# Order edges on VectorE in a hybrid decoder trunk: receptance shifts, score masks and a block inverse

## The chip, the cores and the metric

The kernel runs on one core of a Trainium2 chip. The metric is the device time of one execution in microseconds (us). Before the change it is 1174.61 us, the median of three runs between 1174.42 and 1174.98. The engines are named here as in the profile: PE is TensorE (PEld its weight loads), DVE is VectorE, ACT is ScalarE, POOL is GpSimd, SP issues the DMAs.

## The reference

One decoder layer on 256 tokens of width 2048, in float32. The normed input is multiplied by `w_in`. A quarter of the result goes to a pooling mixer, the rest is shifted by one token and goes to an RWKV-7 mixer with 16 heads of 64, whose state is carried through the sequence:

```
z = rms_norm(x) @ w_in
pool_out = (causal window means of z_pool, minus z_pool) @ pool_w * pool_scale
r, k, v, ... = token_shift(z[rest], mu)          # z + (z_prev - z) * mu
per token and head:  sa = S a;  S = S * w + sa b^T + v k^T;  y = S r
y = group_norm(y) + sum(r * k * r_k) * v          # the bonus
x = x + concat(pool_out, y * g) @ w_out
x = x + relu(rms_norm(x) @ w_ffn_up)^2 @ w_ffn_down
x = x + sigmoid(rms_norm(x) @ w_ple_gate) * (p @ w_ple_proj);  out = rms_norm(x)
```

## The kernel before, in words

**Products.** Every weight is float32 and is split into a high half `wh` (a rounding copy on ScalarE, line 168) and a low half `wl` (the subtraction `raw - wh` on VectorE, line 169); activations are split alike. A product is then three matmuls: high by high (line 244), low activation by high weight (245), high activation by low weight (241). A panel is 128 rows by 1024 columns; `raw`, `wh` and `wl` have three buffers each, so the raw buffer of a panel is free for the third panel after it once its subtraction is done, and its `wl` buffer once its matmuls of line 241 are done. `gemm_toks` is a generator that loads and splits the panels and yields after each step of matmuls. Panels are named by product and number: `zp0_2` is the third of the eight panels of the first pool product.

**The RWKV mixer in chunks.** The recurrence over 256 tokens is done in four chunks of 64 for two groups of eight heads (`gi` 0 and 1). For each group: `rwkv_lora`, `rwkv_k` and `rwkv_r` make the decayed keys, `AR` and `BK`; `rwkv_scores` multiplies them into four groups of scores c0 to c3 (line 672), each in two PSUM banks, and multiplies these by a mask into `SC` (line 679, two instructions for a group); `inverse` inverts triangular blocks of the scores on VectorE; `rwkv_merge` makes two more block products (`gm` and `qm`, line 767) from the inverse's results; `rwkv_values` turns and centres the values (`vt`, line 790), copies them into `UV` (line 793) and makes the bonus; `rwkv_core` runs the recurrence.

**The inverse** is a generator too. It forms `AT`, then takes 31 steps of a multiplication and an addition on `X` (lines 734 and 738), then transposes blocks of `X` into `T1G` (two at line 742), copies (two at 745), transposes back into `X` (two at 749), and ScalarE copies `X` into the scores (line 753). In the first group its tiles `AT`, `X` and `tmp` use the buffers `q0`, `q1` and `q2`. `T1G` takes `q0` when `AT` is done with it, and is read by `gm` and `qm`. The two tiles of `UV` use `q0` and `q1`, so the first half of the values can be copied only when `T1G` is done with, and the second only when `X` is.

**PSUM.** Four banks of the pool "rw" serve everything of the RWKV mixer: the transposed products (`zrT` for the receptance), `vt`, the sums `bsum`, the scores, `gm`, `qm` and the recurrence. The large products have four banks of their own.

**What sets the order.** TensorE's order is that of the program as it is written, through the whole mixer part. `queue` holds the generators of the large products; `fill(us)` takes so many microseconds of their steps to lie between the steps of the RWKV mixer. The inverse of the first group is stepped beside them (`beside`, `pace`), and what is left of it is run out ahead of `rwkv_values(0, ...)`. VectorE and ScalarE are ordered by a planner when the program is built: among the instructions that its own estimate holds ready, it takes the one of highest priority, which is the earlier one in the program, unless it is raised: `high_priority(20000)` for the splits, 30000 for the copies out of PSUM such as the shifts. On the chip each engine keeps the planned order. `issue_after(ins)` puts the instructions of its block behind `ins` on the same engine; `behind` is a table of instructions that others are put behind.

**The receptance shift.** `turn` in `z_product` transposes the product into two banks and calls `shift_evac` for four column groups: ScalarE scales the bank by `1 - mu` into the tile (line 338), VectorE adds the shifted bank times `mu` (line 339).

Of the kernel before, what the change touches and what calls it, by code (L numbers as in the profile page):

```python
# [9 lines left out]
F32 = mybir.dt.float32  # L10
F32R = mybir.dt.float32r
AF = mybir.ActivationFunctionType
ALU = mybir.AluOpType
# [27 lines left out]
def trunk(  # L41
# [119 lines left out]
    def split_w(raw, name, after=None):  # L161

        wh = wp.tile([128, 1024], F32R, tag="wh", name=f"wh_{name}")
        wl = wp.tile([128, 1024], F32R, tag="wl", name=f"wl_{name}")
        with tc.high_priority(20000):
            for a in range(2):
                with tc.issue_after(after.ins) if after is not None else ExitStack():
                    nc.scalar.activation(wh[:, a * 512 : (a + 1) * 512], raw[:, a * 512 : (a + 1) * 512], AF.Copy)  # L168
            nc.vector.tensor_tensor(wl, raw, wh.bitcast(F32), op=ALU.subtract)  # L169
        return [(t_h, t_l) for t_h, t_l in zip((wh[:, 0:512], wh[:, 512:1024]), (wl[:, 0:512], wl[:, 512:1024]))]  # L170

    def split_sb(h_ap, l_ap, src_ap):
# [163 lines left out]

    def shift_evac(dst, src, mu_ap, omu_ap):
        nc.scalar.activation(dst, src, AF.Copy, scale=omu_ap)
        nc.vector.scalar_tensor_tensor(
            dst[:, 1:T], src[:, 0 : T - 1], mu_ap, dst[:, 1:T], op0=ALU.mult, op1=ALU.add  # L340
        )

# [137 lines left out]
    def z_product(i, tag, mu_name, gi, stage="a0"):  # L480

        box = []

        def consume(banks):
            if stage == "a0":
                zt = a8(0, f"{tag}{gi}s")[:, 0:1024].rearrange("p (a n) -> p a n", a=2)
            else:
                zt = rp.tile([128, 2, 512], F32, tag=stage, name=f"{tag}{gi}s")
            with tc.high_priority(30000):
                for tt in range(2):  # L490
                    nc.scalar.activation(zt[:, tt], banks[tt], AF.Copy, scale=rs1[:, tt : tt + 1])
            box.append(zt)

        def turn():
            zt = box.pop()
            dst = e4(tag)
            banks = [rw_bank(f"{tag}T{i}") for i in range(2)]
            for p in range(4):
                for tt in range(2):
                    o = p % 2 * T + tt * 128  # L500
                    nc.tensor.transpose(banks[p // 2][:, o : o + 128], zt[:, tt, p * 128 : (p + 1) * 128], ident)
            for p in range(4):
                c = PARAM_COLS[mu_name] - m0 + 4 * gi + p
                with tc.high_priority(30000):
                    shift_evac(dst[:, p, :], banks[p // 2][:, p % 2 * T : (p % 2 + 1) * T], col(mu_name, 4 * gi + p), omu[:, c : c + 1])
            return dst

        gen = queued(gemm_toks(w_in[i + gi], hT, f"{tag}{gi}", consume))

        def finished(us=1.70):  # L510
            finish(gen)
            fill(us)
            return turn()

        return finished
# [143 lines left out]
    def rwkv_scores(gi, st, cs=(0, 1, 2, 3)):  # L659

        AR, BK = st["AR"], st["BK"]
        if 0 in cs:
            st["SC"] = rp.tile([128, 2, 4, 8, 64], F32, tag="SC", bufs=2, name=f"SC{gi}")
        SC = st["SC"]
        cm = cmask.rearrange("s (k t) -> s k t", k=2)
        for c in cs:
            if c:
                fill(2.60 if gi else 4.55)
            bks = [rw_bank(f"sc{e}") for e in range(2)]
            for p in range(4):  # L670
                for e in range(2):
                    nc.tensor.matmul(
                        bks[e][:, p * 128 : (p + 1) * 128],
                        BK[e * 64 : (e + 1) * 64, p, c].rearrange("p i t -> p (i t)"),
                        AR[e * 64 : (e + 1) * 64, p, c].rearrange("p i t -> p (i t)"),
                        start=True, stop=True,
                    )
            for e in range(2):
                nc.vector.tensor_tensor(
                    SC[:, :, c].rearrange("s k (p e) t -> s k p e t", e=2)[:, :, :, e, :],  # L680
                    bks[e].rearrange("s (p k t) -> s k p t", k=2, t=64),
                    cm.unsqueeze(2).to_broadcast([128, 2, 4, 64]), op=ALU.mult,
                )

    def rwkv_sources(gi, st):

# [14 lines left out]
    def inverse(gi, st):  # L701
# [25 lines left out]
        for k in range(31):  # L727
            n, m = k // 2 + 1, 31 - k
            t_ = X.rearrange("u j t -> u (j t)")[:, 512 : 512 + n * m].rearrange("u (j t) -> u j t", t=m)
            held = {(1, 11): "state1", (1, 16): "state2"}.get((gi, k))  # L730
            while held and held not in behind:
                yield
            with tc.issue_after(behind[held].ins) if held else ExitStack():
# [4 lines left out]
            nc.vector.tensor_tensor(W[:, 0:n, k + 1 : 32], W[:, 0:n, k + 1 : 32], t_, op=ALU.add)  # L738
            yield
        T1G = rp.tile([96, 32, 32], F32, tag=tags[0], name=f"T1G{gi}")  # L740
        for i in range(2):
            nc.vector.transpose(T1G[64:96].rearrange("t u j -> t j u")[:, i::2], W[i * 64 : i * 64 + 32])
            yield
        for i in range(2):
            nc.vector.tensor_copy(tmp[0:64, i::2, :], W[i * 64 : i * 64 + 64])
            yield
        for hf in range(2):
            h = slice(hf * 16, hf * 16 + 16)
            nc.vector.transpose(X[0:64].rearrange("j u t -> j t u")[:, h], tmp[0:64].rearrange("u j t -> u t j")[:, h])
            yield  # L750
        for q in range(2):
            r = slice(q * 32, q * 32 + 32)
            nc.scalar.activation(SCu[r, :, q * 32 : q * 32 + 32], X[r], AF.Copy)
        st["T1G"] = T1G
        yield

    def rwkv_merge(gi, st):
# [22 lines left out]
        fill(4.19 if gi else 1.52)  # L780
        block_products("qm", lambda u: two(T1G[32:64, u]), lambda u: SCu[32:64, u, 32:64], SCu[0:32, :, 32:64])

    def rwkv_values(gi, st, zv):

        uvs = [rp.tile([128, 2, 8, 64], F32, tag=f"q{i}", name=f"UV{gi}_{i}") for i in range(2)]
        UV = [uvs[c // 2][:, c % 2] for c in range(4)]
        for tt in range(2):
            b = rw_bank("vt")
            for p in range(4):
                nc.tensor.matmul(b[:, p * 128 : (p + 1) * 128], zv[:, p, tt * 128 : (tt + 1) * 128], cen, start=True, stop=True)  # L790
            for i in range(2):
                with tc.high_priority(30000):
                    nc.scalar.activation(flat3(UV[2 * tt + i])[64:128], b[i * 64 : (i + 1) * 64, :], AF.Copy)
        bon = st["rk"]
        bf, vf = flat(bon), flat(zv)
        block_sum(
            st["rk"], f"rk{gi}",
            lambda hf, b: nc.vector.tensor_tensor(
                bf[:, hf * 512 : (hf + 1) * 512], b, vf[:, hf * 512 : (hf + 1) * 512], op=ALU.mult
            ),  # L800
        )
        st["UV"] = UV

    def rwkv_core(gi, st, started=None):
        AR, pc, SC, BKt, UV = st["AR"], st["pc"], st["SC"], st["BKt"], st["UV"]
# [244 lines left out]
    st1 = rwkv_lora(1)  # L1050
    rwkv_k(1, st1, z_zk1(1.33))
    rwkv_r(1, st1, z_zr1())
    run(beside.pop(0) if beside else ())
    beside.clear()
    rwkv_values(0, st0, zv0)
    make_bands()
    fill(8.39)
    rwkv_scores(1, st1)
# [18 lines left out]
    run(beside.pop(0) if beside else ())  # L1077
    beside.clear()
    rwkv_merge(1, st1)
    rwkv_values(1, st1, zv1)  # L1080


    xr = [a8(3 + tt, f"x{tt}") for tt in range(2)]
# [484 lines left out]
```

## Time and profile before

| | |
|---|---|
| median of 3 runs | 1174.61 us (1174.42 to 1174.98) |
| the profiled execution: its own time | 1175.37 us |
| the profiled execution: span of the trace | 1173.4 us, 17398 instructions |
| granted TensorE clock | 0.999 |
| HBM read | 221.19 MB, 190 GB/s over the span |

The profile is one execution. Its page gives the busy time of each engine and the chain of work that ended last. The answers of the trace used below are of two kinds. A row of waits reads: engine, what it was about to do and its line, who released it, then the total in us, how often, the longest. A row of a timeline reads: start in us from the span's start, duration, engine, line, operation, output and inputs, shapes and count; where several instructions in a row are merged, the duration runs from the first start to the last end. A bracket behind it gives the idle time of the engine ahead of it and what released it. Consecutive instructions overlap a little, so that the next one starts up to 0.1 us before the last one ends.

The stretch that the change touches lies between 155 and 190 us: the end of the first group's inverse, the second group's keys and receptance, and the second group's scores, beside the first pool product (`zp0`).

### The profile page before, as it was taken

The page shows a single profiled execution, that of the slowest core. Times are in us where ns is not written, and L with a number is a line of the kernel's source. Part 1 is how long each engine was busy: PE and PEld are TensorE (multiplying, and loading weights), DVE is VectorE, ACT ScalarE, POOL GpSimd, SP SyncE. Part 2 cuts the span into 40 slices and gives each one's busy share as a digit, 9 for nine tenths or more (in the row PEclk, how much of TensorE's full clock was granted, in tenths as well). Part 3 has the DMA queues.
Part 4 walks back from the last instruction along what each step waited for, and adds up shares of the span by engine and source line. Part 5 has one row for each costly group of instructions (what it writes and reads, how often), then busy time and mean ns, then how long its engine had stood idle before and what let it go on. Part 6 is the DMA issues. An engine that isn't in the chain of part 4 may idle for free.

```text
span 1173.4 us, 17398 instructions
## 1 busy us (share of the span) xinstructions
PE 1160.2 (99%) x6407; PEld 972.1 (83%) x6407; DVE 877.7 (75%) x1194; ACT 713.5 (61%) x1323; POOL 57.1 (5%) x133
## 2 busy tenths in 40 slices
PE   9999999999999999999999999999999999999997
PEld 8788777888888888888888888888888888888886
DVE  7686996964756666766998997676768988897543
ACT  8776849676544565555664664555556665677543
POOL 2100000000000000000110110000000110000000
PEclk9999999999999999999999999999999999999999
DMA  7454343354455555565786786555555886975511
GB/s 292 154 202 147 131 139 117 129 180 161 161 200 178 180 183 194 197 216 180 223 246 213 229 254 218 193 186 193 184 193 165 260 254 220 323 241 188 197 55 72
DMA packets 67253, 224.42 MB, mean 191 GB/s; under 512 B 7712, under 2 KB 8480, under 8 KB 66784
## 3 DMA queue, kind: packets, MB, share of 16 engines
q1 hardware_dynamic: 60240, 207.38, 51.5%
q0 software_dynamic: 6496, 15.21, 5.7%
q8 instruction: 50, 0.82, 0.3%
q10 hardware_dynamic: 432, 0.73, 0.2%
q14 instruction: 35, 0.29, 0.1%
HBM read 221.19 MB, written 2.10 MB: 190 GB/s over the span
## 4 chain that ended last, share of the span: by engine, by line
PE 96%; DVE 2%; DMA 1%; ACT 1%; issue 0%; POOL 0%; SPq 0%; DVEq 0%; POOLq 0%; ACTq 0%
PE u_w L1136 20%; PE u_w L1141 10%; PE d_b L1293 7%; PE d_b L1295 7%; PE d_b L1294 7%; PE d_w L1293 2%; PE d_w L1295 2%; PE d_w L1294 2%; PE gt_b L244 2%; PE gt_b L245 2%; PE gt_b L241 2%; PE zp_b L241 1%; PE zv_b L244 1%; PE zv_b L241 1%; PE zk_b L244 1%; PE zv_b L245 1%
## 5 line engine op out<-in xcount | busy, mean ns | idle before, releaser
L1136 PE MATMUL u_w<-h,wh_u 128*128 128x512 f32 x1024 | 321.8, 396 | 0.0
L168 ACT ACTIVATE wh_u<-raw_u 128x512 fp32r<-128x512 f32 x256 | 147.5, 624 | 162.8 <-issue 101.8
L169 DVE TENSOR_TENSOR wl_u<-raw_u,wh_u 128x1024 fp32r<-128x1024 f32 x128 | 156.7, 1224 | 104.8 <-ACT wh_u L168 103.3
L1141 PEld LDWEIGHTS u_w<-h,wl_u 128*128 128x128 f32 x1024 | 192.7, 188 | 45.1
L1141 PE MATMUL u_w<-h,wl_u 128*128 128x256 f32 x1024 | 201.2, 278 | 0.0
L1136 PEld LDWEIGHTS u_w<-h,wh_u 128*128 128x128 f32 x1024 | 156.1, 189 | 0.2
L169 DVE TENSOR_TENSOR wl_gt<-raw_gt,wh_gt 128x1024 fp32r<-128x1024 f32 x24 | 29.4, 1224 | 23.2 <-ACT wh_gt L168 23.1
L173 ACT ACTIVATE wad<-ring 128x512 fp32r<-128x512 f32 x29 | 18.2, 628 | 43.9 <-DVE ring L1344 43.9
L168 ACT ACTIVATE wh_gt<-raw_gt 128x512 fp32r<-128x512 f32 x48 | 27.9, 633 | 24.2 <-PE gt_b L245 17.0
L244 PE MATMUL gt_b<-wh_gt,h 128*128 128x512 f32 x96 | 37.4, 390 | 0.0
L245 PE MATMUL gt_b<-wh_gt,h 128*128 128x512 f32 x96 | 37.4, 390 | 0.0
L1346 DVE TENSOR_TENSOR raw_d<-raw_d,ring 128x1024 f32<-128x1024 f32 x29 | 35.5, 1223 | 0.7
L1263 POOL DMA_DIRECT2D ring<-in_w_ffn_down_dram x29 | 16.5, 568 | 362.0 <-DVE wad L174 361.3
L1264 POOL DMA_DIRECT2D ring<-in_w_ffn_down_dram x29 | 25.3, 874 | 105.5 <-DMA ring<-in_w_ffn_down_dram 105.5
L169 DVE TENSOR_TENSOR wl_o<-raw_o,wh_o 128x1024 fp32r<-128x1024 f32 x16 | 19.6, 1223 | 12.9 <-ACT wh_o L168 11.4
L168 ACT ACTIVATE wh_o<-raw_o 128x512 fp32r<-128x512 f32 x32 | 18.4, 623 | 16.3 <-issue 8.5
L168 ACT ACTIVATE wh_zp<-raw_zp 128x512 fp32r<-128x512 f32 x32 | 18.6, 623 | 15.8 <-PE zp_b L245 7.2
L169 DVE TENSOR_TENSOR wl_zk<-raw_zk,wh_zk 128x1024 fp32r<-128x1024 f32 x16 | 19.4, 1222 | 10.2 <-ACT wh_zk L168 10.2
L244 PE MATMUL zv_b<-wh_zv,hTh 128*128 128x512 f32 x64 | 26.0, 406 | 0.0
L241 PE MATMUL gt_b<-wl_gt,h 128*128 128x512 f32 x96 | 25.8, 389 | 0.0
L244 PE MATMUL zp_b<-wh_zp,hTh 128*128 128x512 f32 x64 | 25.7, 401 | 0.0
L168 ACT ACTIVATE wh_zk<-raw_zk 128x512 fp32r<-128x512 f32 x32 | 18.4, 622 | 11.9 <-DMA raw_zk<-in_w_in_dram 5.7
(927 smaller groups left out, 3014.8 us busy)
## 6 DMA issues: line engine op xcount, KB each, us to landing
raw_u<-in_w_ffn_up_dram SPq DMA_DIRECT2D x128, 512.0 KB, 4.3
raw_d<-in_w_ffn_down_dram SPq DMA_DIRECT2D x99, 512.0 KB, 4.7
ring<-in_w_ffn_down_dram POOLq DMA_DIRECT2D x58, 256.0 KB, 4.6
raw_gt<-in_w_ple_gate_dram SPq DMA_DIRECT2D x24, 512.0 KB, 4.1
raw_zk<-in_w_in_dram SPq DMA_DIRECT2D x16, 512.0 KB, 3.8
raw_zr<-in_w_in_dram SPq DMA_DIRECT2D x16, 512.0 KB, 3.2
raw_zv<-in_w_in_dram SPq DMA_DIRECT2D x16, 512.0 KB, 3.3
raw_zp<-in_w_in_dram SPq DMA_DIRECT2D x16, 512.0 KB, 3.3
```

The source lines that it names most:

```text
L168: nc.scalar.activation(wh[:, a * 512 : (a + 1) * 512], raw[:, a * 512 : (a + 1) * 512], AF.Copy)
L169: nc.vector.tensor_tensor(wl, raw, wh.bitcast(F32), op=ALU.subtract)
L241: nc.tensor.matmul(banks[tt], ah[:, ts_], halves[a][1], start=False, stop=last)
L244: nc.tensor.matmul(banks[tt], ah[:, ts_], halves[a][0], start=i + a == 0, stop=False)
L245: nc.tensor.matmul(banks[tt], al[:, ts_], halves[a][0], start=False, stop=False)
L1136: nc.tensor.matmul(bank[:, ct, :].rearrange("p (s t) -> p s t", s=2), wh[:, cs[ct]], hl, start=k == 0, stop=False, skip_group_check=True,)
L1141: nc.tensor.matmul(bank[:, ct, 0:T], wl[:, cs[ct]], hl[:, 0, :], start=False, stop=k == 15, skip_group_check=True)
L1264: nc.gpsimd.dma_start(slot(n), w_down[pair, hf * 16 + kp, 0, :, 1, :], accum_op=ALU.add)
L1293: nc.tensor.matmul(banks[n], ah, wh, start=first, stop=False)
L1294: nc.tensor.matmul(banks[n], ah, wl, start=False, stop=False)
L1295: nc.tensor.matmul(banks[n], al, wh, start=False, stop=last)
L1346: nc.vector.tensor_tensor(t43, t43, t2.unsqueeze(1).to_broadcast([128, 2, 512]), op=ALU.subtract)
```

## The change

It adds order edges, moves one copy and holds one generator back; no arithmetic changes.

- `shift_evac` returns its VectorE instruction. The last receptance shift of the second group is entered as `"zp0_2 low"`, and `split_w` puts the subtraction of the panel of that name behind it.
- `rwkv_scores` of the second group enters its masks as `mask0` to `mask3`, and as the instruction that the subtractions of the pool panels `zp0_5`, `zp0_6`, `zp0_7` and a panel `zp0_8` are put behind (the pool product has panels 0 to 7).
- The first inverse's step 29 is put behind the bonus, its transposes into `T1G` behind `mask0`, and its transposes back into `X` behind `mask1`. It stops where these are not yet in the program.
- `rwkv_values` no longer copies the turned values at once. It emits the bonus, and returns a function that steps the inverse on to a stage, and at stage 3 allocates `UV` and copies the values. For the first group it is called after the bonus and after the masks of c0 and c1.

```diff
-            nc.vector.tensor_tensor(wl, raw, wh.bitcast(F32), op=ALU.subtract)
+            low = behind.get(f"{name} low")
+            with tc.issue_after(low.ins) if low is not None else ExitStack():
+                nc.vector.tensor_tensor(wl, raw, wh.bitcast(F32), op=ALU.subtract)
...
+            if (tag, gi) == ("zr", 1):
+                behind["zp0_2 low"] = moved
...
             for e in range(2):
-                nc.vector.tensor_tensor(
+                masked = nc.vector.tensor_tensor(
...
+            if gi:
+                behind[f"mask{c}"] = behind[f"zp0_{5 + c} low"] = masked
+                if c < 2:
+                    turned0(c + 2)
...
-            held = {(1, 11): "state1", (1, 16): "state2"}.get((gi, k))
+            held = {(0, 29): "bonus", (1, 11): "state1", (1, 16): "state2"}.get((gi, k))
...
+        while not gi and "mask0" not in behind:
+            st["ahead"] = 1
+            yield
         for i in range(2):
-            nc.vector.transpose(T1G[64:96].rearrange("t u j -> t j u")[:, i::2], W[i * 64 : i * 64 + 32])
+            with tc.issue_after(behind["mask0"].ins) if not gi else ExitStack():
+                nc.vector.transpose(T1G[64:96].rearrange("t u j -> t j u")[:, i::2], W[i * 64 : i * 64 + 32])
             yield
...
+        while not gi and "mask1" not in behind:
+            st["ahead"] = 2
+            yield
         for hf in range(2):
             h = slice(hf * 16, hf * 16 + 16)
-            nc.vector.transpose(X[0:64].rearrange("j u t -> j t u")[:, h], tmp[0:64].rearrange("u j t -> u t j")[:, h])
+            with tc.issue_after(behind["mask1"].ins) if not gi else ExitStack():
+                nc.vector.transpose(
+                    X[0:64].rearrange("j u t -> j t u")[:, h], tmp[0:64].rearrange("u j t -> u t j")[:, h]
+                )
             yield
...
+        def evacuate(stage):
+            while inv and st.get("ahead", 0) < stage:
+                next(inv)
+            if stage < 3:
+                return
+            uvs = [rp.tile([128, 2, 8, 64], F32, tag=f"q{i}", name=f"UV{gi}_{i}") for i in range(2)]
+            UV = [uvs[c // 2][:, c % 2] for c in range(4)]
+            for tt, b in enumerate(turned):
+                for i in range(2):
+                    with tc.high_priority(30000):
+                        nc.scalar.activation(flat3(UV[2 * tt + i])[64:128], b[i * 64 : (i + 1) * 64, :], AF.Copy)
+            st["UV"] = UV
+
+        if not gi:
+            evacuate(1)
+        return evacuate
...
-    run(beside.pop(0) if beside else ())
+    inv0 = beside.pop(0)
     beside.clear()
-    rwkv_values(0, st0, zv0)
+    turned0 = rwkv_values(0, st0, zv0, inv0)
```

More of the change, by code (lines that the diff above doesn't have):

```diff
@@ L338, in shift_evac @@
         nc.scalar.activation(dst, src, AF.Copy, scale=omu_ap)
-        nc.vector.scalar_tensor_tensor(
+        return nc.vector.scalar_tensor_tensor(
             dst[:, 1:T], src[:, 0 : T - 1], mu_ap, dst[:, 1:T], op0=ALU.mult, op1=ALU.add
@@ L504, in turn @@
                 with tc.high_priority(30000):
-                    shift_evac(dst[:, p, :], banks[p // 2][:, p % 2 * T : (p % 2 + 1) * T], col(mu_name, 4 * gi + p), omu[:, c : c + 1])
+                    moved = shift_evac(dst[:, p, :], banks[p // 2][:, p % 2 * T : (p % 2 + 1) * T], col(mu_name, 4 * gi + p), omu[:, c : c + 1])
+            if (tag, gi) == ("zr", 1):
+                behind["zp0_2 low"] = moved
             return dst
@@ L753, in inverse @@
             nc.scalar.activation(SCu[r, :, q * 32 : q * 32 + 32], X[r], AF.Copy)
-        st["T1G"] = T1G
+        st["T1G"], st["ahead"] = T1G, 3
         yield
@@ L781, in rwkv_merge, with rwkv_values @@
         block_products("qm", lambda u: two(T1G[32:64, u]), lambda u: SCu[32:64, u, 32:64], SCu[0:32, :, 32:64])
-    def rwkv_values(gi, st, zv):
-        uvs = [rp.tile([128, 2, 8, 64], F32, tag=f"q{i}", name=f"UV{gi}_{i}") for i in range(2)]
-        UV = [uvs[c // 2][:, c % 2] for c in range(4)]
+    def rwkv_values(gi, st, zv, inv=None):
+        turned = []
         for tt in range(2):
@@ L790, in rwkv_values, with weighted @@
                 nc.tensor.matmul(b[:, p * 128 : (p + 1) * 128], zv[:, p, tt * 128 : (tt + 1) * 128], cen, start=True, stop=True)
-            for i in range(2):
-                with tc.high_priority(30000):
-                    nc.scalar.activation(flat3(UV[2 * tt + i])[64:128], b[i * 64 : (i + 1) * 64, :], AF.Copy)
+            turned.append(b)
         bon = st["rk"]
         bf, vf = flat(bon), flat(zv)
[L796 to L802, printed above, removed]
+        def weighted(hf, b):
+            cols = slice(hf * 512, (hf + 1) * 512)
+            behind["bonus"] = nc.vector.tensor_tensor(bf[:, cols], b, vf[:, cols], op=ALU.mult)
+        block_sum(st["rk"], f"rk{gi}", weighted)
+        def evacuate(stage):
[13 more added lines that the diff above has]
+        return evacuate
     def rwkv_core(gi, st, started=None):
@@ L1079, in trunk @@
     rwkv_merge(1, st1)
-    rwkv_values(1, st1, zv1)
+    rwkv_values(1, st1, zv1)(3)
     xr = [a8(3 + tt, f"x{tt}") for tt in range(2)]
```

## The prediction

> **What bounds the kernel now.** I read the page first: busy times, then the chain that ended last.
>
> ```profile
> PE 1160.2 (99%) x6407; PEld 972.1 (83%) x6407; DVE 877.7 (75%) x1194; ACT 713.5 (61%) x1323; POOL 57.1 (5%) x133
> PE 96%; DVE 2%; DMA 1%; ACT 1%; issue 0%; POOL 0%; SPq 0%; DVEq 0%; POOLq 0%; ACTq 0%
> ```
>
> TensorE is busy 99% of the span and carries 96% of the chain. The change neither adds nor removes a matmul, and TensorE's order is written by hand, so the change can only move the end by removing or adding TensorE waits. The list of TensorE's waits is therefore the next view; it has five rows, of which these are the three longest:
>
> ```profile
> PE wagT L467 <- POOL wband L132: 1.5, 1, 1.5
> PE rbank L403 <- DVE ones L98: 1.2, 1, 1.2
> PE bsum L526 <- DVE zr_t L339: 1.0, 1, 1.0
> ```
>
> The first two lie in the head of the kernel, ahead of everything the diff touches. The third is in reach: the block sum of the first group's bonus (L526) waits for a receptance shift (L339). TensorE's timeline gives the place:
>
> ```profile
> 156.48 1.95 PE L790 MATMUL vt<-cen,zv_t 128*128 128x128 f32 x16
> 159.44 1.96 PE L526 MATMUL bsum<-ybuf,jsum 128*128 128x512 f32 x4 [1.01 <-DVE zr_t L339]
> ```
>
> Why does a sum over `ybuf` wait for `zr_t`? It reads nothing of it. The pool of "rw" banks has four, and at that moment two hold the transposed receptance (`zrT`) and two the turned values (`vt`). The block sum gets a bank when the shifts have emptied one. So the ceiling of any gain here is 1.01 us, 0.09% of the span. About 0.2% (2.3 us) is what a measurement of this kernel can tell from no change.
>
> **Part one: the shifts ahead of the third pool panel's low half.** VectorE's and ScalarE's timelines at this place:
>
> ```profile
> 155.95 1.22 DVE L169 TENSOR_TENSOR wl_zp<-raw_zp,wh_zp 128x1024 fp32r<-128x1024 f32 x1
> ...
> 157.51 0.47 DVE L339 SCALAR_TENSOR_TENSOR zr_t<-zrT,par_sb,zr_t 128x255 f32<-128x255 f32 x1
> ...
> 158.43 0.87 DVE L339 SCALAR_TENSOR_TENSOR zr_t<-zrT,par_sb,zr_t 128x255 f32<-128x255 f32 x2
> ```
>
> ```profile
> 156.34 0.46 ACT L338 ACTIVATE zr_t<-zrT,omu 128x256 f32<-128x256 f32 x1
> 156.70 0.62 ACT L168 ACTIVATE wh_zp<-raw_zp 128x512 fp32r<-128x512 f32 x1
> 157.22 0.47 ACT L338 ACTIVATE zr_t<-zrT,omu 128x256 f32<-128x256 f32 x1
> 158.02 0.47 ACT L338 ACTIVATE zr_t<-zrT,omu 128x256 f32<-128x256 f32 x1 [0.34 <-DVE zr_t L339]
> 158.94 0.47 ACT L338 ACTIVATE zr_t<-zrT,omu 128x256 f32<-128x256 f32 x1 [0.44 <-DVE zr_t L339]
> ```
>
> The third panel's subtraction holds VectorE from 155.95 to 157.1, so the first shift starts at 157.51, though its ScalarE half was done at 156.80 (156.34 + 0.46). The third ScalarE half starts 0.04 after the first shift ends (157.51 + 0.47 = 157.98), and the fourth 0.04 after the second shift (158.43 + 0.47 = 158.90). I read this as each bank being emptied in turns: ScalarE, VectorE, ScalarE, VectorE, the first and third halves in one bank, the second and fourth in the other. The bank that the block sum takes is free when the third shift ends, at 158.43 + 0.87 = 159.30; TensorE starts 0.14 later, at 159.44.
>
> With the subtraction behind the last shift: first shift 156.84 to 157.31; second ScalarE half unmoved at 157.22 (it follows the `wh_zp` half, which does not move), to 157.69; third half right behind it, to about 158.1; second shift 157.73 to 158.20; third 158.14 to 158.61. The bank is free 0.69 us sooner, so the block sum starts at 158.75. **Part one: -0.69 us.** The bounds are -1.01 (the whole wait) and 0 (if the queue puts other work ahead of the shifts).
>
> What pays for it? The fourth half and shift follow in the other bank, to about 159.2, and the displaced subtraction runs behind them. Its user on TensorE and the loads that take its buffer:
>
> ```profile
> 166.71 1.07 PE L241 MATMUL zp_b<-wl_zp,hTh 128*128 128x512 f32 x4
> raw_zp<-in_w_in_dram SPq DMA_DIRECT2D x16, 512.0 KB, 3.3
> ```
>
> It ends about 160.4, six microseconds ahead of its matmuls. The raw buffer that it frees is refilled in 3.3, so the panel three on has landed by about 164, before its own split. I cost it at nothing; that cover is gone only if it slips by more than 5 us.
>
> **Part two: the masks.** Four score groups, c0 to c3, are each followed by two masks on VectorE:
>
> ```profile
> 169.75 1.16 PE L672 MATMUL sc<-AR,BK 64*128 64x128 f32 x16
> 173.79 1.25 PE L672 MATMUL sc<-AR,BK 64*128 64x128 f32 x16
> 177.91 1.16 PE L672 MATMUL sc<-AR,BK 64*128 64x128 f32 x16
> 181.94 1.16 PE L672 MATMUL sc<-AR,BK 64*128 64x128 f32 x16
> 183.04 1.15 PE L767 MATMUL gm<-T1G,tmp 32*64 32x64 f32 x32
> ```
>
> ```profile
> 164.86 1.13 DVE L742 STREAM_TRANSPOSE T1G<-X 32x512 f32<-32x512 f32 x1
> 166.02 1.23 DVE L169 TENSOR_TENSOR wl_zp<-raw_zp,wh_zp 128x1024 fp32r<-128x1024 f32 x1
> 167.28 1.13 DVE L742 STREAM_TRANSPOSE T1G<-X 32x512 f32<-32x512 f32 x1
> 168.42 0.85 DVE L745 COPY tmp<-X 64x512 f32<-64x512 f32 x2
> 169.31 1.17 DVE L749 STREAM_TRANSPOSE X<-tmp 64x512 f32<-64x512 f32 x1
> 170.39 1.17 DVE L169 TENSOR_TENSOR wl_zp<-raw_zp,wh_zp 128x1024 fp32r<-128x1024 f32 x1
> 171.49 1.19 DVE L749 STREAM_TRANSPOSE X<-tmp 64x512 f32<-64x512 f32 x1
> 172.58 1.25 DVE L679 TENSOR_TENSOR SC<-sc,cmask 128x512 f32<-128x512 f32 x2
> 173.74 1.22 DVE L169 TENSOR_TENSOR wl_zp<-raw_zp,wh_zp 128x1024 fp32r<-128x1024 f32 x1
> 174.98 1.29 DVE L679 TENSOR_TENSOR SC<-sc,cmask 128x512 f32<-128x512 f32 x2
> 183.14 1.29 DVE L679 TENSOR_TENSOR SC<-sc,cmask 128x512 f32<-128x512 f32 x2 [1.08 <-PE sc L672]
> ```
>
> Here is what would be late next if part one stood alone. Group c1 takes 1.25 where the others take 1.16: it starts at 173.79 in banks that the c0 masks leave at 173.83 (172.58 + 1.25). There is no slack, and no wait is marked in VectorE's rows from 164.86 to c1's masks. Without part two the 0.69 would be lost again at c1. With it, c0's masks run as soon as c0 is done: masks start 1.20 after their group (183.14 - 181.94), so at 169.75 - 0.69 + 1.20 = 170.26, and c1 finds its banks in time.
>
> The price is in what is queued behind. VectorE now has to wait for c0 with both T1G transposes behind it, where today they run from 164.86. From 170.26 on, by the starts of the rows above: c0 masks 1.16 (172.58 to 173.74), a pool panel's subtraction 1.24 (173.74 to 174.98), the two T1G transposes 1.16 and 1.14, the copies 0.89, c1 masks 1.16, the next subtraction 1.24 (both subtractions are of raised priority, held only by their masks), the two L749 transposes 1.08 and 1.09: together 10.16, so the inverse ends on VectorE at 180.42, not at 172.68. Only then do c2's masks run, to 180.42 + 1.25 = 181.67. Group c3 is due at 181.94 - 0.69 = 181.25 and needs both banks: **+0.45**, with the few hundredths that TensorE takes to start.
>
> Next, `gm`, which follows c3 at once and needs a bank too. ScalarE's rows show who holds the other two:
>
> ```profile
> 172.77 2.13 ACT L753 ACTIVATE SC<-X 32x1024 f32<-32x1024 f32 x2 [1.95 <-DVE X L749]
> 175.34 1.19 ACT L793 ACTIVATE UV<-vt 64x512 f32<-64x512 f32 x2
> 187.96 1.21 ACT L793 ACTIVATE UV<-vt 64x512 f32<-64x512 f32 x2
> ```
>
> One `vt` bank is emptied at 187.96, after `gm`, since its target shares a buffer with T1G; the other once the L753 copies have read X, at 175.34 to 176.53 today. After the change those copies start at about 180.6 (1.28 after the second L749 transpose starts, as today), and 2.57 later, as today (172.77 to 175.34), that evacuation starts: the bank comes free at about 184.4, or 184.0 without what lies between. So at c3's end all four banks are taken, and the first to come free is that of c3's first mask: c3 starts at 181.70, masks 1.20 later, the first of two done after some 0.69 (more than half of 1.29, for the two overlap), TensorE at about 183.65. `gm` was due at 183.04 - 0.69 + 0.45 = 182.80: **+0.85**. The bounds of this second price are 0 (the `vt` bank is free in time) and 1.6 (it comes from `vt` at 184.4). The other moved pieces cost nothing: the two subtractions end at about 172.7 and 178.3, and TensorE takes them up only just ahead of c2 and c3 (177.91 and 181.94 today), over 2.5 us later, and the longer hold on ScalarE is covered by its waits in that stretch.
>
> The Trainium skill has a rule against this part: PSUM — Partial Sum Buffer, section "Engine vs sequencer instructions", says that the queues of ScalarE, VectorE and GpSimdE are strict FIFO. By it a transpose that is ready cannot pass a mask that waits, and the sum is the one here; if it could pass, the inverse would end as early as today and the sum would stay at part one's gain. No row of this trace shows an instruction passing a waiting one.
>
> **Sum:** -0.69 + 0.45 + 0.85 = +0.61 us. The profiled execution took 1175.37 us with a span of 1173.4, so 1.97 lie around the span and it is 0.76 above the median of the three runs, 1174.61. I expect a span of 1174.0 and put the sum on the median: 1175.2.
>
> **The rivals.** *The gain stays.* If the second subtraction is queued behind the L749 transposes, these end 1.24 sooner, the `vt` bank is free at about 182.8 to 183.2, when `gm` is due, and only c3's 0.45 is paid: -0.24, 1174.4. If c2's masks slip in ahead as well, all of part one stays: 1173.9. For it: the edges name exactly the pieces that could delay the masks. Against it: those subtractions have a raised priority and are ready.
>
> *Slower: an unheld subtraction takes the masks' place.* The fourth edge names a ninth pool panel, and there are only eight; the next panel, zv's first, has no edge. If its subtraction (1.24) falls ahead of c2's masks, c3 waits 0.45 + 1.24: -0.69 + 1.69 + 0.85 = +1.85, 1176.5. It decides if that panel is split by 180.4, and today it is not far off:
>
> ```profile
> 179.67 1.14 ACT L168 ACTIVATE wh_zv<-raw_zv 128x512 fp32r<-128x512 f32 x2
> ```
>
> The late evacuation of `vt` (1.19) can then also fall ahead of the T1G copies, and the recurrence starts that much later: 1177.7.
>
> *The change doesn't do what it says:* the shifts stay where they are because something else fills VectorE. Then the banks cost 1.30 against nothing: 1175.9.
>
> **How the numbers follow.** Forecast 0.42, gain stays 0.32, unheld subtraction 0.17 (0.06 of it with the later start), shifts unmoved 0.09. The range 1173.8 to 1176.6 takes in all but the further slow case and the edges. Faster by over 0.2% needs 2.3 us where the ceiling is 1.01: 0.02 for a side effect on later orders. Slower by over 0.2% is the late start, 0.06. Within 0.2%: 0.92.
>
> **What would show it.** In the changed profile: the wait of the block sum on `zr_t` is down from 1.01 to about 0.3; VectorE is idle for some 4 us ahead of c0's masks; the L749 transposes end near 180.4; new TensorE waits stand at c3 (0.45) and at `gm` (0.85). A row of no waits at c3 and `gm` makes the first rival right; wl_zv ahead of c2's masks the second; a block sum still at 159.4 the third.

## The result and the profile after

The changed kernel takes 1177.84 us (median of 21 runs, 1176.06 to 1179.09). The kernel before, run in turn with it, takes 1175.42 us (21 runs, 1174.42 to 1177.78). The ratio is 1.0013, with a 95% interval of 1.0008 to 1.0019: slower by some 1.5 us, between 0.9 and 2.2. (The two medians lie further apart, 2.42, because the run times fall in two groups not quite 2 us apart, clearly so in the changed kernel and less sharply in the one before, and the medians fall into different ones; the last section shows the groups.) That is on the forecast's side of zero, but larger than its +0.61, and 1177.84 lies above the range. The median of before rose by 0.81 as well, from 1174.61 in the first three runs.

The first view of the changed kernel is the page's line of busy times:

```profile
PE 1161.3 (99%) x6407; PEld 972.0 (83%) x6407; DVE 877.7 (75%) x1194; ACT 714.4 (61%) x1323; POOL 58.3 (5%) x133
```

Each engine's count of instructions is that of before, and the other engines' busy times barely differ. What was moved is order, so what changed must be waits. TensorE's list of waits in the changed kernel (us in total, times, longest):

```profile
PE wag_b L398 <- ACT wagh L384: 1.9, 1, 1.9
...
PE gm L785 <- ACT UV L828: 1.1, 1, 1.1
...
PE qm L785 <- ACT T1G L792: 0.4, 1, 0.4
PE bsum L530 <- DVE zr_t L341: 0.3, 1, 0.3
```

The block sum's wait fell from 1.01 to 0.3. Two waits are new: `gm` for the copies of the turned values (`UV`), and `qm` for the copies into `T1G`. The head's rows vary too: `wag_b` waits 1.9 here and is not among the five rows of before. Such waits lie ahead of the change and differ between executions of one kernel (`wag_b` waits 0.9 in e11 and 0.7 in e12, below), so absolute times mislead. From here on places on TensorE are counted from the first `zrT` transpose, which stands at 155.61 in the trace of before and 157.26 in that of after. TensorE's timeline of the changed kernel (start, busy time, and in brackets the idle time before it and its releaser):

```profile
157.26 1.03 PE L503 MATMUL zrT<-ident,zr1s 128*128 128x128 f32 x8
...
160.42 1.96 PE L530 MATMUL bsum<-ybuf,jsum 128*128 128x512 f32 x4 [0.34 <-DVE zr_t L341]
...
182.86 1.16 PE L676 MATMUL sc<-AR,BK 64*128 64x128 f32 x16
185.11 1.15 PE L785 MATMUL gm<-T1G,tmp 32*64 32x64 f32 x32 [1.09 <-ACT UV L828]
...
188.73 1.14 PE L785 MATMUL qm<-SC,T1G 32*64 32x64 f32 x30 [0.41 <-ACT T1G L792]
```

The place of each step, from `zrT`, in us, and how far the changed kernel's lies from it:

| | bsum | c0 | c1 | c2 | c3 | gm | qm, first | qm, last | rym | um | last matmul |
|---|---|---|---|---|---|---|---|---|---|---|---|
| before | 3.83 | 14.14 | 18.18 | 22.30 | 26.34 | 27.43 | 30.32 | 31.25 | 34.79 | 36.76 | 1009.54 |
| after | -0.67 | -0.66 | -0.66 | -0.74 | -0.74 | +0.42 | +0.42 | +1.14 | +1.16 | +1.16 | +1.21 |

Read along a row, each step between neighbours is one gain or one loss. The gain of 0.67 is kept up to c3; `gm` loses 1.16 and `qm` 0.72; nothing after `um` adds more than 0.1. Two further executions of the same kernel (e11 and e12, below) give +0.41 and +0.43 at `gm`, +1.24 and +1.26 at the end.

VectorE's timeline of the changed kernel shows the order that the edges made:

```profile
168.99 0.86 DVE L757 COPY tmp<-X 64x512 f32<-64x512 f32 x2
171.93 1.29 DVE L683 TENSOR_TENSOR SC<-sc,cmask 128x512 f32<-128x512 f32 x2 [2.08 <-PE sc L676]
...
174.38 2.23 DVE L754 STREAM_TRANSPOSE T1G<-X 32x512 f32<-32x512 f32 x2
176.64 1.29 DVE L683 TENSOR_TENSOR SC<-sc,cmask 128x512 f32<-128x512 f32 x2
...
178.98 2.23 DVE L765 STREAM_TRANSPOSE X<-tmp 64x512 f32<-64x512 f32 x2
181.11 1.24 DVE L683 TENSOR_TENSOR SC<-sc,cmask 128x512 f32<-128x512 f32 x2
182.28 1.20 DVE L171 TENSOR_TENSOR wl_zp<-raw_zp,wh_zp 128x1024 fp32r<-128x1024 f32 x1
183.41 1.21 DVE L171 TENSOR_TENSOR wl_zv<-raw_zv,wh_zv 128x1024 fp32r<-128x1024 f32 x1
184.54 1.27 DVE L683 TENSOR_TENSOR SC<-sc,cmask 128x512 f32<-128x512 f32 x2
```

VectorE stands idle for 2.08 ahead of c0's masks, with the transposes of the inverse queued behind them. The last pair of them now starts 21.72 after `zrT` (178.98 - 157.26) instead of 13.70 (169.31 - 155.61). c2's masks (181.11) stand right behind them and are done at 182.35, half a microsecond ahead of c3 (182.86). ScalarE's timeline shows what the late inverse does there:

```profile
181.30 2.13 ACT L771 ACTIVATE SC<-X 32x1024 f32<-32x1024 f32 x2 [1.45 <-DVE X L765]
...
183.87 1.19 ACT L828 ACTIVATE UV<-vt 64x512 f32<-64x512 f32 x2
...
185.68 1.14 ACT L168 ACTIVATE wh_zv<-raw_zv 128x512 fp32r<-128x512 f32 x2
...
187.12 1.55 ACT L792 ACTIVATE T1G<-gm 32x256 f32<-32x256 f32 x4
...
194.72 0.78 ACT L859 ACTIVATE R<-rym 64x256 f32<-64x256 f32 x2
```

From 181.30 on no row is marked with idle time, up to the evacuation of `R` at 194.72 (the rows left out among the first ones are pieces of `BK`). The copies of X, the evacuation of the `vt` bank, the split of zv's second panel and the copies into `T1G` follow each other. `gm` starts when the evacuation is done (185.06), and `qm` starts when the copies of its operands are far enough.

The same rows hold a limit that TensorE's waits do not show. From the start of the copies of X to `R` ScalarE works for 13.42 us without a pause (181.30 to 194.72). Before, these copies started at 172.77 and `R` was evacuated at:

```profile
191.83 0.78 ACT L828 ACTIVATE R<-rym 64x256 f32<-64x256 f32 x2
```

That is 19.06 for the same way, 5.64 more than now, with idle time in it (and with some other small pieces). The copies of X now start 6.88 later (24.04 from `zrT` instead of 17.16), more than those 5.64 can take up, so `R` comes 1.24 later (37.46 instead of 36.22). In this order on ScalarE it could come no sooner, however little TensorE waits; `um`, which reads `R`, is 1.16 later.

### The profile page after: what moved, and what is told of

The parts are those of the page before. It is cut to its first block, busy times and chain, and to the rows that moved or that the text cites. A ratio compares the mean times of both kernels' runs of the same rounds, so it can differ in the third digit from the quotient of the medians.

```text
span 1176.3 us, 17397 instructions
## 1 busy us (share of the span) xinstructions
PE 1161.3 (99%) x6407; PEld 972.0 (83%) x6407; DVE 877.7 (75%) x1194; ACT 714.4 (61%) x1323; POOL 58.3 (5%) x133
## 4 chain that ended last, share of the span: by engine, by line
PE 95%; DVE 2%; ACT 1%; DMA 1%; issue 0%; SPq 0%; POOL 0%; DVEq 0%; ACTq 0%; POOLq 0%
PE u_w L1167 20%; PE u_w L1172 10%; PE d_b L1324 7%; PE d_b L1326 7%; PE d_b L1325 7%; PE d_w L1326 2%; PE d_w L1324 2%; PE d_w L1325 2%; PE gt_b L246 2%; PE gt_b L243 2%; PE gt_b L247 2%; PE zv_b L246 1%; PE zv_b L243 1%; PE zk_b L246 1%; PE zk_b L247 1%; PE zv_b L247 1%
## 5 line engine op out<-in xcount | busy, mean ns | idle before, releaser
L246 PE MATMUL zk_b<-wh_zk,hTh 128*128 128x512 f32 x64 | 25.9, 405 | 0.0
```

Of the source, the lines that this page charges most:

```text
L246: nc.tensor.matmul(banks[tt], ah[:, ts_], halves[a][0], start=i + a == 0, stop=False)
```

## The experiments

The theory after this reading: the loss is the late end of the inverse, which the edges behind c0's and c1's masks make. It is paid first in a bank that `vt` holds, then in ScalarE's queue. The rivals: the bank alone; the order of the copies and the split on ScalarE alone; part one. e5 and e8 were timed in eleven runs each. Every other variant ran once, and one time cannot be read against a scatter of 3 us (1176.06 to 1179.09 for the changed kernel), so the places are what counts.

### e1: part one alone

```diff
 (before, with)
+            low = behind.get(f"{name} low")
+            with tc.issue_after(low.ins) if low is not None else ExitStack():
                 nc.vector.tensor_tensor(wl, raw, wh.bitcast(F32), op=ALU.subtract)
...
+            if (tag, gi) == ("zr", 1):
+                behind["zp0_2 low"] = moved
```

> The kernel before with one edge alone: the third pool panel's subtraction behind the last receptance shift. Places are counted on TensorE from the first transpose of the receptance (zrT), so that the head of the kernel is left out: before, the block sum starts 3.83 us after it, c0 14.14, c1 18.18, gm 27.43. Theory A (the edge does what it says): block sum at 3.2, as in the changed kernel, and the 0.67 is lost again at c1, whose banks the masks leave no sooner; the end unmoved, 0.0 to -0.1. Theory B (the place in VectorE's queue that the subtraction leaves goes to the inverse, which comes earlier in the program): the T1G transposes run between the shifts, block sum at about 5.3, both bonus products behind the inverse, so that c0 waits for their banks; the end about 2.2 later.

Measured: 1178.6 us beside 1176.51 of before on the same chip; the block sum +1.30, c0 +1.65, c1 +3.40, the last matmul +3.29. VectorE's timeline of e1 shows why the edge on its own is worse than none:

```profile
156.94 1.07 DVE L746 STREAM_TRANSPOSE T1G<-X 32x512 f32<-32x512 f32 x1
158.05 0.48 DVE L341 SCALAR_TENSOR_TENSOR zr_t<-zrT,par_sb,zr_t 128x255 f32<-128x255 f32 x1
158.56 1.04 DVE L746 STREAM_TRANSPOSE T1G<-X 32x512 f32<-32x512 f32 x1
...
170.61 0.65 DVE L802 TENSOR_TENSOR ybuf<-bsum,zv_t 128x512 f32<-128x512 f32 x1
...
172.31 0.68 DVE L802 TENSOR_TENSOR ybuf<-bsum,zv_t 128x512 f32<-128x512 f32 x1
```

With the subtraction held back, pieces of the inverse move up into its place, and one T1G transpose stands ahead of the first shift and one between the first and second. The products of the bonus (L802), which empty the block sum's banks, slip behind the end of the inverse; c0 waits for them 0.30 and 1.25. This is theory B, wait at c0 included; only its size was off, +3.3 for the 2.2 expected. So part one needs something that holds the inverse back. The edge that puts its step 29 behind the bonus is enough: e5 and e9 below have no edge on the T1G transposes and keep the -0.67, which is the work of both edges together.

### e2: part two alone

```diff
 (after, without)
-            if (tag, gi) == ("zr", 1):
-                behind["zp0_2 low"] = moved
```

> The changed kernel without the edge on the third panel's subtraction; masks, inverse and values as changed. If the chain behind c0 hangs on c0 itself (masks, transposes, copies, vt bank), all of it moves with c0: block sum at 3.8 from zrT, gm waits 1.1 as in the changed kernel, and the end is 0.67 later than there, +1.9 against before. If that chain hangs on VectorE's work ahead of c0, its end stays where it is: gm waits about 0.4 and the end is +1.2, as in the changed kernel.

Measured: 1177.14 us; the block sum -0.22, c0 -0.23, c3 -0.31, `gm` +0.85 with the same wait of 1.09 for the same evacuation, `qm` +2.37, the last matmul +2.05. `gm` loses 1.16 here as in the changed kernel, so its wait is part two's and moves with the chain. At `qm` there is no wait; the rest is TensorE's own speed. TensorE by windows in e2 (us, busy time and instructions, granted clock, DMA share, GB/s):

```profile
184.00:188.00 4.00, 4.00 (x34) 0.57 0.56 192
188.00:192.00 4.00, 4.00 (x46) 1.00 0.38 133
```

A granted clock of 0.57 over 4 us is half speed for 0.43 x 2 x 4 = 3.4 us. From `gm` to `qm` e2 takes 4.41 (183.59 to 188.00) where before takes 2.89 (30.32 - 27.43): 1.52 lost. This was in no expectation. It does not follow that the end would lie 1.52 sooner at full speed: in e2 too ScalarE has no idle time from the copies of X (24.47 from `zrT`) to `R` (37.91), and `um` follows `R` by at least 0.43 in every variant. That alone puts `um` at some +1.6, an estimate from these rows: the +1.16 of the changed kernel, later by about the 0.43 by which c0 is later here. So the chain hangs on c0, the first of the two cases expected.

### e3: `gm` in a bank of the other pool

```diff
 (after, with)
-            b = rw_bank(name)
+            b = mm_bank(name) if (gi, name) == (0, "gm") else rw_bank(name)
```

> The changed kernel with gm's result in a bank of the large products' pool; the order on every engine is that of the changed kernel. If gm waits for the bank of the turned values (theory of the prediction), its wait of 1.09 is gone and it starts 26.7 after zrT, not 27.85. If it waits for its own inputs (the late T1G transposes, the copies), nothing moves. In either case the copies of gm's result stand behind the copies of the values and a split of zv's second panel on ScalarE, at the same time as now, so qm should wait the longer (1.4 in place of 0.41) and the end stay at +1.1 to +1.2: the late inverse is then paid for twice over, and taking one wait away gains nothing.

Measured: `gm` does not wait at all (-0.74, as c3), and `qm` waits instead. TensorE's list of waits in e3, and its windows behind them:

```profile
PE qm L785 <- ACT T1G L792: 1.5, 2, 1.0
```

```profile
184.00:188.00 4.00, 2.52 (x36) 0.83 0.70 221
188.00:192.00 4.00, 4.00 (x11) 0.50 0.07 29
192.00:196.00 4.00, 4.00 (x33) 0.82 0.00 0
```

The bank's part is shown: `gm`'s wait was for a bank, since a bank of the other pool removes all of it. But the copies into `T1G` still stand behind the `UV` copies and the split on ScalarE, and the time returns one step later, 1.01 + 0.47. The expectation was 1.4 for it. On top comes half speed for 6.8 us by the windows, which makes the way from the last `qm` to `rym` 6.18 instead of 3.54: the end at +3.97, the time 1178.61. `R` waits 2.36 for `rym` here; ScalarE was ready for it at 192.27, 37.41 from `zrT`. By that the end at full speed would be at the +1.1 to +1.2 that was expected.

### e4 and e7: the split behind the copies into `T1G`

```diff
 (after, with; e7 has e3's line as well)
-                    nc.scalar.activation(place[:, r::4], src, AF.Copy)
+                    copied = nc.scalar.activation(place[:, r::4], src, AF.Copy)
+            if (gi, name) == (0, "gm"):
+                behind["zv1_1"] = copied
```

> The changed kernel with the split of zv's second panel on ScalarE put behind the four copies of gm's result. The wait of gm (1.09) stays; the copies start as soon as gm is done, 0.85 sooner than now, and qm's wait of 0.41 is gone. End at +0.4 to +0.5 against before, in place of +1.21. If the 0.7 lost at qm have another cause (a bank for qm, the inverse's copies into the scores), the end stays at +1.2.

> The changed kernel with both: gm's result in a bank of the other pool, and the split of zv's second panel behind the copies of gm's result. gm does not wait (26.7 from zrT); the copies still stand behind the late copies of the inverse and of the values on ScalarE, so that qm's second half waits some 0.4. End at -0.2 to -0.3 against before. If the two waits had other causes than bank and ScalarE order, the end stays at +0.4 or above.

Measured in e4: `gm` waits 1.09 as before the edit, `qm` not at all (+0.42 at its last matmul), so the split's place in the queue was `qm`'s wait. Yet the last matmul is at +1.49, the time 1176.49 us: the +0.4 to +0.5 that was expected is missed. Measured in e7: `gm` free, `qm` waits 0.5, the end at +1.2 a hundred microseconds on (and 1.84 at the last matmul, after another wait far behind), 1178.66 us; -0.2 to -0.3 was expected. The list of waits of e4, then of e7:

```profile
PE gm L785 <- ACT UV L830: 1.1, 1, 1.1
PE um L900 <- ACT R L861: 0.8, 1, 0.8
```

```profile
PE um L900 <- ACT R L861: 0.9, 1, 0.9
...
PE sm L914 <- ACT UV L904: 0.7, 1, 0.7
PE qm L785 <- ACT T1G L792: 0.5, 1, 0.5
```

The wait is carried on, from `qm` to `um`, whose operand `R` ScalarE evacuates. ScalarE's queue from the end of the inverse to `R` is full, so what is put behind one copy stands ahead of the next: from the copies of X to `R` it takes 13.42 in e7 as in the changed kernel, and 13.65 in e4, where ScalarE stood idle for 0.24 until `gm` was done. `R` is at 37.68 from `zrT` in e4 and at 37.42 in e7, where the changed kernel has 37.46, so neither could gain more than a few hundredths at `um`. The wait at `sm` in e7 is another matter. It lies 120 us on, and the evacuation that it waits for stands behind a copy on ScalarE that waited for a load:

```profile
277.36 1.16 ACT L175 ACTIVATE pws<-raw_pw 128x512 fp32r<-128x512 f32 x2 [1.00 <-DMA raw_pw<-in_pool_w_dram]
```

None of the orders and banks tried here repairs an inverse that ends late.

### e9 and e10: each of the two edges undone alone

```diff
 (e9: after, with the T1G transposes free)
-        while not gi and "mask0" not in behind:
-            st["ahead"] = 1
-            yield
         for i in range(2):
-            with tc.issue_after(behind["mask0"].ins) if not gi else ExitStack():
-                nc.vector.transpose(T1G[64:96]...)
+            nc.vector.transpose(T1G[64:96]...)
...
-            evacuate(1)
+            evacuate(2)
```

```diff
 (e10: after, with the transposes back behind c0's masks)
-        while not gi and "mask1" not in behind:
-            st["ahead"] = 2
-            yield
...
-            with tc.issue_after(behind["mask1"].ins) if not gi else ExitStack():
+            with tc.issue_after(behind["mask0"].ins) if not gi else ExitStack():
                 nc.vector.transpose(X[0:64]...)
```

In e10 the inverse is stepped to its end after c0 (`if c == 0: turned0(3)`).

> The changed kernel with the T1G transposes free of the edge to c0's masks; the transposes back stay behind c1's masks, and the values are copied after them. By TensorE's places from zrT: c1's masks then start with c1's end, 0.6 sooner than in the changed kernel, and all behind them is 0.6 sooner. If the loss comes mainly from the edge on the transposes back: gm waits about 0.5 in place of 1.09, the end is at +0.5 to +0.6 against before. If it comes mainly from the edge on the T1G transposes: no wait at gm, end at -0.7.

> The changed kernel with the transposes back behind c0's masks (not c1's), the T1G transposes behind c0's masks as now, and the values copied behind c0. VectorE then does all four transposes between the masks of c0 and c1. gm should not wait, for the inverse ends 2.4 sooner; but c1's masks end 3.4 after they do now, at 22.7 from zrT, and c2, due at 21.56, needs their banks: c2 at about 22.7, end at +0.4 to +0.5. If it is the edge on the transposes back alone that costs, c2 does not wait and the end is at -0.7.

Measured in e9: `gm` -0.31, last `qm` +0.41, +0.48 a hundred microseconds on and +0.33 at the last matmul; 1175.33 us beside 1177.08 of before. Measured in e10: c2 -0.06, c3 and all behind it +0.54 to +0.58; 1175.71 us. TensorE's waits there, e9 and then e10, and VectorE's rows of e10:

```profile
PE qm L781 <- ACT T1G L788: 0.4, 1, 0.4
PE gm L781 <- ACT UV L824: 0.4, 1, 0.4
```

```profile
PE sc L676 <- DVE SC L683: 0.6, 1, 0.6
```

```profile
172.44 2.24 DVE L754 STREAM_TRANSPOSE T1G<-X 32x512 f32<-32x512 f32 x2
174.69 2.27 DVE L762 STREAM_TRANSPOSE X<-tmp 64x512 f32<-64x512 f32 x2
176.87 1.23 DVE L683 TENSOR_TENSOR SC<-sc,cmask 128x512 f32<-128x512 f32 x2
```

In e9 the idle 2.08 is filled, and ScalarE's copies of X start 0.73 sooner (23.31 from `zrT`, against 24.04). `gm`'s wait shrinks to 0.4 and `qm`'s stays at 0.4: the edge behind c1's masks is left, and the +0.5 to +0.6 that was expected is about met. ScalarE again takes 13.42 from the copies of X to `R`, which is 0.51 later than before (36.73 from `zrT`). In e10 that edge is gone, and `gm`, `qm` and `um` wait for nothing. But c1's masks come too late for c2, because both pairs of transposes, 4.5 together, now stand between the masks of c0 and c1: c2 waits 0.62 for its first bank and then takes 1.75 instead of 1.16, which I read as the wait for its second, and c3 and all behind it are late by that. The end is about as expected (+0.4 to +0.5). Each edge has a price of its own.

### e5 and e8: both edges undone, and one more held piece

```diff
 (e5: e9's first hunk, e10's change, and)
-                if c < 2:
-                    turned0(c + 2)
+                if c == 0:
+                    turned0(3)
```

```diff
 (e8: e5, with the fourth panel's split behind the ScalarE halves of the shifts)
-        nc.scalar.activation(dst, src, AF.Copy, scale=omu_ap)
+        behind["shift half"] = nc.scalar.activation(dst, src, AF.Copy, scale=omu_ap)
...
+                behind["zp0_3"] = behind["shift half"]
```

> The changed kernel with the inverse held back less: the T1G transposes have no edge, the transposes back stand behind c0's masks (not c1's), and the values are copied behind c0. VectorE then has the T1G transposes in the 2 us in which it now waits for c0, the inverse ends some 4.6 us sooner, the vt bank is free about 4 us ahead of gm. Theory (the loss is the late inverse alone): no wait at gm or qm, the block sum's gain of 0.67 stays, end at -0.67 against before (ratio 0.9994). Rival (holding the values behind the scores costs by itself, by ScalarE's order or by the banks of c2 and c3): waits at c2, c3 or um, end at 0 or above.

> As the kernel with the inverse held back less, and the split of the fourth pool panel on ScalarE behind the four receptance halves, where one half of it now stands between them. The block sum still waits 0.34 there: without the split between, the third half starts when the first shift ends, and the sum starts some 0.3 sooner, 2.85 from zrT; end at -0.95 to -1.0 against before. If the wait that is left comes from the turns of the two engines in one bank alone, nothing moves, -0.67.

Measured in e5: -0.75 from c2 to `um` (-0.67 was expected), and -0.95 at the last matmul. TensorE's whole list of waits has four rows, three of them of the head:

```profile
PE wagT L469 <- POOL wband L131: 1.2, 1, 1.2
PE rbank L405 <- DVE ones L98: 1.2, 1, 1.2
PE zkT L503 <- ACT zk1s L493: 0.8, 2, 0.5
PE bsum L530 <- DVE zr_t L341: 0.3, 1, 0.3
```

VectorE's rows of e5, where the T1G transposes fill the gap ahead of c0's masks:

```profile
168.22 2.23 DVE L750 STREAM_TRANSPOSE T1G<-X 32x512 f32<-32x512 f32 x2
170.46 0.85 DVE L753 COPY tmp<-X 64x512 f32<-64x512 f32 x2
171.34 1.29 DVE L683 TENSOR_TENSOR SC<-sc,cmask 128x512 f32<-128x512 f32 x2
...
173.68 2.19 DVE L761 STREAM_TRANSPOSE X<-tmp 64x512 f32<-64x512 f32 x2
175.75 1.27 DVE L683 TENSOR_TENSOR SC<-sc,cmask 128x512 f32<-128x512 f32 x2
```

c0's masks and c1's both come in time, and the last pair of transposes starts 17.19 after `zrT` (173.68 - 156.49) instead of 21.72. This is the test that tells the theory from its rivals: no bank is changed and the split has no new edge, and the waits at `gm` and `qm` are gone. The copies of the values do move, from behind c1 to behind c0, but they need the buffers of T1G and X and so follow the end of the inverse in any case. e8 takes the block sum's wait from 0.34 to 0.17, and the gain to -0.92 up to `um` and -1.07 at the last matmul (expected: -0.95 to -1.0).

On the clock, e5 takes 1174.97 us (11 runs) and e8 1173.93 (11 runs) beside 1175.28 of before (21 runs): both ratios 0.9992, with intervals of 0.9983 to 1.0002 and 0.9983 to 1.0001. The traces put both ahead of before by 0.75 to 1.07; the times agree with that but cannot tell it from nothing.

### e11 and e12: the changed kernel twice more

> The changed kernel as it is, profiled once more, for the granted clock. In the runs so far TensorE had a stretch of 3.41 us at half speed in the head of some executions (head to zrT 155.3 to 156.1) and none in others (153.7 to 154.4), and one behind gm's wait in two of the variants. If that is a matter of where the wait falls, this execution has the same places from zrT to qm's start (gm at 27.85, end +1.21) and may have a half-speed stretch behind gm or not; with one the end is at about +2.9. If the +1.21 is not fixed by the order, the places differ.

> As the one before it: places to qm's start unchanged, end at +1.21 without and about +2.9 with a half-speed stretch behind gm's wait.

Both are the changed kernel unaltered. They take 1178.31 and 1176.19 us on one chip, yet from `zrT` on their places agree within 0.06. The 2.12 between the times lies ahead of it: first matmul to `zrT` takes 156.09 in e11 and 153.96 in e12. TensorE's windows there, e11 and then e12:

```profile
36.00:40.00 4.00, 2.35 (x11) 0.78 0.42 143
40.00:44.00 4.00, 4.00 (x16) 0.79 0.20 44
```

```profile
36.00:40.00 4.00, 3.15 (x20) 1.00 0.42 140
...
```

e11 ran (0.22 + 0.21) x 2 x 4 = 3.4 us at half speed there; e12 did not.

## Why the prediction was right or wrong

**Part one, -0.69.** Right: -0.67, by the predicted way, the block sum's wait falling to 0.3. What it did not say is that a second edge, the bonus ahead of step 29, is needed for it (e1).

**c3, +0.45.** Wrong: no wait at c3. The further gain of 0.07 comes earlier, between c1 and c2, and stems from c1's slow run in the trace of before (1.25 where the others take 1.16). The working put the two copies (0.89) behind c0's masks. No edge holds them, and they ran ahead, in VectorE's idle time (168.99). From the first of c0's masks to the first of c2's it takes 9.18 (171.93 to 181.11), 10.37 from c0 itself, where the sum had 11.36. VectorE was idle for 2.08, not 4, because these copies and the inverse's last two steps (168.11 to 168.95), held back behind the bonus, ran in the time that was to be idle.

**`gm`, +0.85.** Right in kind, too small: +1.16. The place, the four taken banks and both candidates to come free were named. The working took c3's first mask as the first; it was `vt`, at 185.06, since two subtractions, `wl_zp` and `wl_zv`, stood ahead of c3's masks on VectorE. `wl_zv` is the unheld panel of the second rival, one place later than that rival had it. The value is inside the bounds of 0 to 1.6. That the bank decides is shown by e3.

**`qm`, 0.** This is the step that failed: "the longer hold on ScalarE is covered by its waits in that stretch". It was not. The idle times that were to cover it lie ahead of 181.30 (the last is the 1.45 in that row); behind it ScalarE has none until `R`, and the copies into `T1G` start 0.86 after `gm` ends (187.12 against 186.26). The piece ahead of them that makes `qm` wait is the split of zv's second panel at 185.68, for with that split put behind them in e4 the wait is gone. It cost +0.72, where the sum had nothing; the nearest case, the late evacuation ahead of these copies, had a chance of 0.06. e4 and e7 show that the cover is missing in the whole chain, not at one copy: ScalarE's 13.42 from the copies of X to `R` put `R` 1.24 later than before, a limit that the prediction did not add up.

**The sum.** -0.67 - 0.07 + 1.16 + 0.72 + 0.07 at and behind `rym` = +1.21, where +0.61 was forecast: the gain right, one cost not there, one mis-sized and one missing. That the sum is only 0.60 off is in part luck: c3's 0.45 that did not come offsets part of the 1.03 too little at `gm` and `qm`. The time is 2.64 above the forecast of 1175.2: 0.81 of that is the risen median of before, and most of the rest is the two groups of run times. That a measurement cannot tell less than 0.2% (2.3 us) from no change was too cautious: 21 runs against 21 do so for 1.5 us. The timed difference is +1.5 (0.9 to 2.2), with which +1.21 agrees. What lies between them, if it is anything, stays open: half-speed stretches behind the waits, as in e2 and e3, would make it, but none of the three traces of the changed kernel has one there.

**The rivals.** That the gain stays fell: the subtractions did stay ahead of the L765 transposes. That the edges do nothing fell. The slower rival named the right panel, in another place: ahead of c3's masks rather than c2's, so that it cost nothing at c3. c3's masks start at 184.54 instead of 1.20 after c3, at 184.06, which is a price of some 0.3 at `gm` (an estimate: the first mask would then have freed its bank at about 184.75). Of the signs, the block sum's wait held; the idle time (2.08 for 4) and the wait at c3 (none for 0.45) did not. The transposes' end, 181.21, is 23.95 from `zrT`; forecast was 180.42, 24.81 from the 155.61 of before.

**The rule on queues.** The prediction set its sum by the rule that ScalarE's and VectorE's queues are first in, first out (the Trainium skill, PSUM — Partial Sum Buffer, "Engine vs sequencer instructions"). This case agrees: the T1G transposes, whose X was ready when the copies of the same X ran at 168.99, ran at 174.38 behind masks that waited until 171.93.

## What to carry to other kernels

An order edge prices the whole chain behind the held piece, down to the last engine with no idle time: follow that chain row by row, and take cover only from idle time that lies behind the new start, not ahead of it. Where the engine that serves the chain is full, moving its pieces among themselves only moved the wait (`qm` to `um`); add up its work from the held piece's end to the first result that the critical engine needs. What helped, in the traces of e5, was to hold nothing back that could run in the idle time in front of the edge, and to place one pair of transposes per gap. To compare executions that differ by less than their heads do, count places from one instruction in front of the change.

## What was not expected of the hardware

TensorE's granted clock was halved in single stretches of some 3.4 us. One cost 1.52 between `gm` and `qm` in e2, two cost 2.64 between `qm` and `rym` in e3. They came behind a wait of 1.09 in e2 (one stretch) and of 1.01 and 0.47 in e3 (two, 6.8 us). They did not come behind 2.31 and 1.25 in e1, nor behind the 1.09 and 0.41 of the changed kernel. So the length of a wait alone does not decide. Nor does TensorE's busy share: it is busy for 2.31 of 3.40 us both in e2 (181.20 to 184.60, with a stretch behind) and in the changed kernel (181.80 to 185.20, with none). That it depends on where the wait falls is possible and not shown. The Trainium skill, TensorE: Matmul & The Clock Gate, section "Part 1: The HAM clock gate", says that the clock halves after an idle window of about 3.4 us and that this window runs freely. The length of the stretches agrees; in e2 the wait ahead of one was only 1.09.

In the head the same stretch comes in some executions of one kernel and not in others (at some 38 to 42 us in e5, e7, e8 and e11, at 8 to 11 in the profiled execution of the changed kernel): the head takes 155.3 to 156.1 us in the five traces that have one and 153.7 to 154.4 in the eight that have none. This would be most of the scatter of the run times. The 21 runs of the changed kernel fall in two groups, 1176.06 to 1176.96 and 1177.84 to 1179.09, and the profiled e12 and e11 fall one into each. The mean granted clock of each run fits: 0.998 in all ten of the lower group, 0.995 to 0.997 in ten of the eleven of the upper one. A median over few runs can land in either group, which is what the 0.81 between the two medians of before looks like.
